# Attention weights turned as pairs of 64 rows, in a two-layer retention and neighbourhood-attention transformer

## The chip, the cores and the metric

The kernel runs on one NeuronCore of a Trainium2 chip. The metric is the device time of one execution in microseconds; a kernel's time is the median of several executions. The core has five engines that work side by side and wait for each other by semaphores: TensorE (PE in the profile; its weight loads are PEld), VectorE (DVE), ScalarE (ACT), GpSimd (POOL) and SyncE (SP, which here only issues loads). TensorE writes to PSUM, which has eight banks of 512 fp32 columns on 128 partitions; VectorE and ScalarE take results out of it.

## What is computed

A transformer of two layers on 256 latent and 256 context tokens of width 1024. Layer 0 mixes by retention, layer 1 by attention: 32 heads of width 32, where each latent token attends to a window of latent tokens with a learned bias and to all context tokens. An MLP of width 4096 follows each mixer, with layer norms and modulation in between. The part that matters here, cut from the reference:

```python
def row_block(args):
    q_r, r = args
    ...
    s_loc = jnp.einsum('bqhd,bikhd->bhqik', q_r, k_band).astype(jnp.float32) + bias
    s_ctx = jnp.einsum('bqhd,blhd->bhql', q_r, k_c).astype(jnp.float32)
    s = jnp.concatenate([s_loc.reshape(b, nh, GRID_W, band), s_ctx], axis=-1)
    prob = jax.nn.softmax(s, axis=-1).astype(v.dtype)
    p_loc = prob[..., :band].reshape(b, nh, GRID_W, kh, GRID_W)
    return (jnp.einsum('bhqik,bikhd->bqhd', p_loc, v_band)
            + jnp.einsum('bhql,blhd->bqhd', prob[..., band:], v_c))
```

## The kernel before

Every matrix product is done to nearly fp32 precision by three TensorE passes (`mm3`): each operand is rounded to fp32r (`hi`, by ScalarE) and the rest is kept (`lo`, by subtraction on VectorE or GpSimd), and hi x hi, hi x lo and lo x hi are summed in PSUM. Weights come as units of 512 KB: `fetch` issues SP's load into one of four `raw` buffers and ScalarE's rounding, `lows` the subtraction. A unit is usable when both are done, and its `raw` buffer is free for another load then.

The attention of layer 1 is cut into 16 tiles, n = 0 to 15: four heads (group n // 2) and half of the queries (128 of 256; n % 2). A tile passes through these stages:

- `scores(n)`: TensorE multiplies queries by keys for four heads side by side, 32 rows of the array each, into four PSUM banks (`pqk`).
- `soften(n)`: for each head VectorE adds the bias to the scores and takes the minimum (scores are negated), and ScalarE takes the exponential and its sum, into `s` in SBUF (128 queries x 416 keys: 160 near, 256 far). Its end issues the bias load of tile n+2 on GpSimd's queue.
- `invert(n)`: VectorE takes the reciprocals of the sums and spreads them (`rr`).
- the turn, `flip_near(n)` and `flip_far(n)`: TensorE transposes the weights (`ppt`), keys to the partitions. The near part is turned in halves of 64 queries: eight transposes of 64 rows, two row halves of the array at a time, into two banks. The far part is eight transposes of 128 rows into two more banks, and `rr` is transposed (one of 128 rows) into the right half of attend's bank. ScalarE copies one near and one far bank to SBUF, VectorE the others. `turned(n)` is ScalarE's copy of the turned reciprocals, at the head of the next step.
- `attend(n)`: TensorE multiplies the turned weights by the values (`pav`, 32 columns of the array for each head), VectorE multiplies by the reciprocals (`rt`), ScalarE rounds the result (`oTh`) and VectorE subtracts (`oTl`).

The loop over `STEPS` (lines 1893 to 1917) runs these as a pipeline: step n does the scores and softening of tile n+2, one block of other TensorE work (`before`: a group of keys `K`, queries `Q`, a quarter of the second half's values `V`, or the first half of an output projection `W`), the turn of tile n+1 and attend of tile n. `before` leaves a function that takes its result out of PSUM (`evac`; for keys two ScalarE roundings and two VectorE subtractions), run between the near and the far part. The step's entry names its weight units: `early` ahead of the scores, `late` behind the softening, `last` at the end. In steps 1 to 8 their subtractions are GpSimd's, later mostly VectorE's.

In this stretch TensorE, VectorE, ScalarE and GpSimd are held to the order in which the program is written (`on`: each instruction is pinned behind the one written before it on its engine); the pinning of ScalarE lasts beyond the loop, to the first blocks of the MLP. A bank or a buffer is taken by the next tile when the last reader of the one before has finished. One bank is attend's throughout, a second from step 13, and the output projections hold one each from their block on.

Of the kernel before, what the change touches and what calls it, by code (L numbers as in the profile page):

```python
# [10 lines left out]
F32 = mybir.dt.float32  # L11
# [6 lines left out]
P = 128  # L18
# [75 lines left out]
def kernel(  # L94
# [23 lines left out]
    pe, act, dve, pool, sp = (  # L118
        InOrder(tc, getattr(nc, e), e in PIN)
        for e in ("tensor", "scalar", "vector", "gpsimd", "sync")  # L120
    )
# [3 lines left out]
    smp = ec(tc.tile_pool(name="smp", bufs=4))  # L125
# [15 lines left out]
    def nm(s):  # L141
        uid[0] += 1
        return f"{s}_{uid[0]}"

    def bank(s="ps"):
        return psp.tile([P, 512], F32, tag="ps", name=nm(s))
# [8 lines left out]
    def tsl(t):  # L155
        return slice(t * P, (t + 1) * P)
# [82 lines left out]
    def fetch(n, home=None):  # L239

        for src, k, ncol in specs[len(units) : len(units) + max(n, 0)]:
            raw = rawp.tile([P, k, ncol], F32, tag="raw", name=nm("raw"))
            sp.dma_start(out=raw[:], in_=src.rearrange("(k p) n -> p k n", p=P))
            if home is None:
                hi = hip.tile([P, k, ncol], F32R, tag="hi", name=nm("hi"))
                lo = lop.tile([P, k, ncol], F32R, tag="lo", name=nm("lo"))
            else:
                both_ = slot(home, [P, 2, k, ncol], F32R, "unit")
                hi, lo = both_[:, 0], both_[:, 1]
            act.copy(out=hi[:], in_=raw[:])  # L250
            pending.append((lo[:], raw[:], hi[:]))
            units.append((hi, lo))
# [23 lines left out]
    def lows(n=100, eng=None):  # L276
        for lo, raw, hi in pending[:n]:
            (eng or dve).tensor_sub(out=lo, in0=raw, in1=hi.bitcast(F32))
        del pending[:n]
# [21 lines left out]
    def cv(name, p0=0, p1=P):  # L301
        o, w = CONST_COLS[name]
        if o < NC0:
            return cst0[p0:p1, o : o + w]
        return cst1[p0:p1, o - NC0 : o - NC0 + w]

    ident = cv("ident")
# [403 lines left out]
    def residual(t, xn, gb, eng=None):  # L711
        if eng:
            eng.tensor_mul(out=R[t], in0=xn, in1=gb[:, 0, :])
            eng.tensor_add(out=R[t], in0=R[t], in1=gb[:, 1, :])
            return
        pool.on = True
        pool.tensor_mul(out=R[t], in0=xn, in1=gb[:, 0, :])
        pool.tensor_add(out=R[t], in0=R[t], in1=gb[:, 1, :])
        pool.on = False
# [218 lines left out]
    for i in range(4):  # L938
        k = 2 * i
# [140 lines left out]
    for h in range(RH):  # L1080
# [11 lines left out]
        else:  # L1092
# [13 lines left out]
            for u in range(4):  # L1106
                ((wh, wl),) = take(1)
                for t in range(4):
                    for kk in range(2):
                        k = 2 * u + kk  # L1110
# [75 lines left out]
        for t in range(4):  # L1186
            po = bank("po")
            scs = list(range(4)) if t < 2 else [2, 3]
            for i, sc in enumerate(scs):
                a, b = S[sc]  # L1190
# [8 lines left out]
                out=on, in0=po[:], scalar1=mv[:, 0:1], scalar2=r[:], op0=ALU.subtract, op1=ALU.mult  # L1199
# [7 lines left out]
        def to_oT(t):  # L1207
            pT = bank("pT")
            for i in range(4):
                pe.transpose(pT[:, tsl(i)], gs[:, t, tsl(i)], ident)  # L1210
            pv_ = pT[:].rearrange("p (k t) -> p k t", k=4)
            act.copy(out=oh[:, :, tsl(t)], in_=pv_)
            dve.tensor_sub(out=ol[:, :, tsl(t)], in0=pv_, in1=oh[:, :, tsl(t)].bitcast(F32))

        between = {4: lambda: to_oT(0), 5: lambda: to_oT(1)}
# [31 lines left out]
        else:  # L1247
# [17 lines left out]
            def turn(t):  # L1265
                return [mod_pt(xns[t], half) for half in range(2)]
# [78 lines left out]
    for hf in range(2):  # L1345
# [60 lines left out]
        for half in range(2):  # L1406
# [68 lines left out]
            p = turn(0)  # L1475
# [9 lines left out]
            p = turn(1)  # L1485
# [13 lines left out]
    NS = 16  # L1499
# [117 lines left out]
    NEARK, FARK = NEAR * ROWS, NLAT  # L1617
# [18 lines left out]
    sums, rrs, Es, pss = {}, {}, {}, {}  # L1636

    def scores(n):

        g, qt = n // 2, n % 2  # L1640
        pss[n] = [bank("pqk") for _ in range(4)]
        q, k = q_of(g), kTs[g // 2][:, g % 2]
        if qt == 0:
            spans = [(0, slice(0, NEARK)), (NEARK, slice(NLAT, NT))]
        else:
            spans = [(0, slice(NLAT - NEARK, NT))]
        for o, keys in spans:
            for i, (a, b) in enumerate(((0, 0), (0, 1), (1, 0))):
                for j in range(4):
                    js = slice(32 * j, 32 * j + 32)  # L1650
                    pe.matmul(
                        pss[n][j][:, o : o + keys.stop - keys.start], lhsT=q[js, a, tsl(qt)], rhs=k[js, b, keys],
                        start=(i == 0), stop=(i == 2), tile_position=(32 * j, 0),
                    )
# [28 lines left out]
    def av_half(n):  # L1683
        return av[n == NS - 2][:, 256 * (n % 2) : 256 * (n % 2) + 256]

    def invert(n):

        rr = rrs[n] = smp.tile([P, 4, HD], F32, tag="rr", name=nm("rr"), bufs=1)
        dve.reciprocal(out=sums[n][:], in_=sums[n][:])
        dve.tensor_copy(out=rr[:], in_=sums[n][:].unsqueeze(2).broadcast_to([P, 4, HD]))  # L1690

    def near_part(n):
        return turnedP[n % 2][:, :512].rearrange("p (a h t) -> p a h t", a=2, h=4)

    def far_part(n):
        return turnedP[n % 2][:, 512:1536].rearrange("p (h k t) -> p h k t", h=4, k=2)

    def flip_near(n):
        pn = [bank("ppt") for _ in range(2)]
        for j in range(4):  # L1700
            for a in range(2):
                qs = slice(64 * a, 64 * a + 64)
                pe.transpose(
                    pn[a][:, 64 * j : 64 * j + 64], Es[n, j][qs, 32 * a : 32 * a + P], ident[qs, qs],
                    tile_position=(64 * a, 0),
                )
        for a in range(2):
            (dve.tensor_copy if a else act.copy)(
                out=near_part(n)[:, a], in_=pn[a][:, :256].rearrange("p (h t) -> p h t", h=4)
            )  # L1710

    def flip_far(n):
        for a in range(2):
            pf = bank("ppt")
            for i in range(4):
                c0 = NEARK + P * (i % 2)
                pe.transpose(pf[:, tsl(i)], Es[n, 2 * a + i // 2][:, c0 : c0 + P], ident)
            (dve.tensor_copy if a else act.copy)(
                out=far_part(n)[:, 2 * a : 2 * a + 2], in_=pf[:].rearrange("p (h k t) -> p h k t", h=2, k=2)
            )  # L1720
        pe.transpose(av_half(n)[:, P:], rrs[n][:].rearrange("p h d -> p (h d)"), ident)

    oTs = [None]
    rts = {}

    def turned(n):

        rts[n] = smp.tile([P, P], F32, tag="rt", name=nm("rt"), bufs=2)
        act.copy(out=rts[n][:], in_=av_half(n)[:, P:])

    def attend(n, between=lambda: None):

# [39 lines left out]
    def wo_add(half, t):  # L1772
        add_to(t, half, gated(wops[half, t], t, half, G1), dve)
# [65 lines left out]
    soften(1)  # L1839
    v_part(0, 1)  # L1840
    invert(0)
    flip_near(0)
    flip_far(0)
    residual(1, xns[1], gb, dve)
    regrid()
    v_part(0, 2)
# [10 lines left out]
    def Q(p):  # L1857
        def f():
            for u in range(2):
                q_mm(p, u)  # L1860
            return lambda: q_evac(p)

        return f
# [18 lines left out]
        ((), (), W01, (None,)),  # L1882
        ((), (), W10, ()),
    ]
    pool.on = True

    def weights(homes, eng=None):
        for home in homes:
            fetch(1, home)
            if eng:  # L1890
                lows(1, eng)

    for n, (early, late, before, last) in enumerate(STEPS):
        turned(n)
        weights(early, pool if n else None)
        scores(n + 2)
        soften(n + 2, lambda: lows(0 if n else 1))
        if n > 9:
            lows(1)
        weights(late, pool if n < 9 else dve if n == 9 else None)  # L1900
        if n == 9:
            Q(3)()()
            weights((None,), dve)
        evac = before()
        flip_near(n + 1)
        if evac:
            evac()
        if n == NS - 3:
            av[1] = bank("pav")
        flip_far(n + 1)  # L1910
        if n == NS - 3:
            turned(n + 1)
        attend(n)
        invert(n + 2)
        if n == 10:
            wo_add(0, 0)
        weights(last, pool if n < 9 else None)


    n = NS - 1  # L1920
    st1 = small(smp, 24, "st1", name="st1", bufs=1).rearrange("p (q s) -> p q s", q=4)
    weights((N_Q, N_B))
    attend(n - 1, lambda: lows(1))
    flip_near(n)
    flip_far(n)
    turned(n)
    lows(2)
    us = take(4, 0)
    gb = slot(N_K1, [P, 2, D], F32, "gb")
# [302 lines left out]
```

## Time and profile before

| what | us |
|---|---|
| median of 3 runs | 1175.21 (1174.76 to 1175.26) |
| the profiled execution, device time | 1176.4 |
| its span, first to last instruction | 1174.6 |
| TensorE busy | 1162.7 |
| VectorE busy | 812.9 |
| ScalarE busy | 480.3 |
| GpSimd busy | 145.3 |

The attention loop runs from 842.96 us (scores of tile 2) to about 964.8 us of the span, the turn of the first tile stands ahead of it at 830.54 us, that of the last behind it at 965.69 us. A row of the timeline reads: start, length, engine, line, operation, what is written from what, partitions and elements, count; in brackets the time that the engine stood idle before it and what ended that. Consecutive instructions of one kind are merged in one row, so a row's length is from the first one's start to the last one's end; matmuls overlap, and the distance between starts is their pace. All lines are L84, the helper that pins instructions, so groups are told apart by their tiles.

### The profile page before, as it was taken

Reading aid. Unit: us, or ns where it says so; the run is one execution under the profiler, and the core shown is the slowest. Engines: PE = TensorE matmul, PEld = TensorE weight load, DVE = VectorE, ACT = ScalarE, POOL = GpSimd, SP = SyncE. Lnnn points to the kernel's source line nnn. Section 1 sums busy time; section 2 is a strip of 40 time slices with the busy share of each in tenths; the row PEclk is TensorE's granted clock in tenths of the full one; section 3 lists DMA queues with packets and bytes.
Section 4 is the critical chain, followed back from the end, with each engine's and each line's share of the span. In section 5 each row is a group of like instructions: output and inputs, shape, how many; then the busy total and the mean of one; then the engine's idle time right before and its main releaser. Section 6 shows DMA issues by size and latency. Waiting matters only on the chain.

```text
span 1174.6 us, 17876 instructions
## 1 busy us (share of the span) xinstructions
PE 1162.7 (99%) x7042; PEld 982.2 (84%) x7042; DVE 812.9 (69%) x1286; ACT 480.3 (41%) x816; POOL 145.3 (12%) x168
## 2 busy tenths in 40 slices
PE   9999999999999999999999999999999999999997
PEld 6788888888888889888788878889778879999886
DVE  3575896689697376468888665578465588877555
ACT  3643442143323245232222433237466675655450
POOL 0102002100200240000202000140245300000000
PEclk9999999999999999999999999999999999999999
DMA  9742552857255214347675655646634543676861
GB/s 322 233 135 79 162 177 77 288 154 220 85 158 189 76 57 133 79 119 226 233 228 180 199 192 183 197 143 197 200 110 150 168 132 120 202 242 220 289 218 37
DMA packets 134468, 199.99 MB, mean 170 GB/s; under 512 B 16192, under 2 KB 76384, under 8 KB 134384
## 3 DMA queue, kind: packets, MB, share of 16 engines
q1 hardware_dynamic: 129696, 185.64, 49.9%
q0 software_dynamic: 3296, 10.55, 2.9%
q10 hardware_dynamic: 1392, 2.67, 0.6%
q8 instruction: 55, 0.90, 0.3%
q14 instruction: 29, 0.24, 0.1%
HBM read 190.31 MB, written 10.61 MB: 171 GB/s over the span
## 4 chain that ended last, share of the span: by engine, by line
PE 92%; DVE 4%; DMA 2%; ACT 1%; issue 1%; DVEq 0%; ACTq 0%; SPq 0%
PE p L84 39%; PE pw L84 7%; PE pv L84 7%; PE pq L84 7%; PE pg L84 7%; PE pn L84 6%; PE pnv L84 4%; PE po L84 3%; PE pnw L84 2%; PE ppt L84 2%; PE pS L84 1%; DVE acc L84 1%; PE pav L84 1%; PE pqk L84 1%; PE pt L84 1%; DMA rawa<-in_ada_w_dram 1%
## 5 line engine op out<-in xcount | busy, mean ns | idle before, releaser
L84 ACT CAST hi<-raw 128x1024 fp32r<-128x1024 f32 (+1 forms) x222 | 220.7, 1011 | 287.1 <-DMA raw<-in_mlp_w_dram 118.2
L84 DVE TENSOR_TENSOR lo<-raw,hi 128x1024 fp32r<-128x1024 f32 (+1 forms) x211 | 247.0, 1184 | 86.9 <-ACT hi L84 85.2
L84 PE MATMUL p<-hi,hid 128*128 128x512 f32 (+1 forms) x792 | 230.9, 373 | 0.0
L84 PE MATMUL p<-hTh,hi 128*128 128x256 f32 (+1 forms) x512 | 168.6, 330 | 0.0
L84 PE MATMUL p<-hTh,lo 128*128 128x256 f32 (+1 forms) x512 | 168.1, 330 | 0.4 <-DVE lo L84 0.4
L84 PEld LDWEIGHTS p<-hi,hid 128*128 128x128 f32 x792 | 144.9, 188 | 26.2
L84 PE MATMUL p<-hTl,hi 128*128 128x256 f32 (+1 forms) x512 | 166.2, 329 | 0.0
L84 PE MATMUL p<-lo,hid 128*128 128x512 f32 (+1 forms) x396 | 147.4, 372 | 0.0
L84 DVE SCALAR_TENSOR_TENSOR acc<-rawa,scol,acc 128x1024 f32<-128x1024 f32 x63 | 83.4, 1344 | 44.7 <-DMA rawa<-in_ada_w_dram 44.6
L84 PEld LDWEIGHTS p<-hTh,lo 128*128 128x128 f32 x512 | 97.3, 190 | 9.6 <-DVE lo L84 0.9
L84 PEld LDWEIGHTS p<-hTh,hi 128*128 128x128 f32 x512 | 97.3, 190 | 8.7
L84 PEld LDWEIGHTS p<-hTl,hi 128*128 128x128 f32 x512 | 96.3, 190 | 8.7
L84 PEld LDWEIGHTS p<-lo,hid 128*128 128x128 f32 x396 | 74.6, 188 | 12.9
L84 ACT CAST hid<-r 128x512 fp32r<-128x512 f32 (+1 forms) x60 | 31.2, 520 | 108.2 <-DVE r L84 108.1
L84 DVE SCALAR_TENSOR_TENSOR strips<-rawa,scol,strips 128x512 f32<-128x512 f32 x84 | 57.5, 744 | 0.0
L84 DVE TENSOR_TENSOR hid<-r,hid 128x512 fp32r<-128x512 f32 (+1 forms) x60 | 33.8, 563 | 25.5 <-ACT hid L84 25.5
L84 PE MATMUL pw<-hi,oh 128*128 128x512 f32 x128 | 50.9, 398 | 0.0
L84 PE MATMUL pg<-hi,hTh 128*128 128x512 f32 x128 | 50.7, 396 | 0.0
L84 PE MATMUL pv<-hi,hTh 128*128 128x512 f32 x128 | 50.4, 394 | 0.0
L84 PE MATMUL pw<-hi,ol 128*128 128x512 f32 x128 | 49.9, 390 | 0.0
L84 PE MATMUL pg<-hi,hTl 128*128 128x512 f32 x128 | 49.9, 390 | 0.0
L84 PE MATMUL pv<-hi,hTl 128*128 128x512 f32 x128 | 49.9, 390 | 0.0
(234 smaller groups left out, 2200.3 us busy)
## 6 DMA issues: line engine op xcount, KB each, us to landing
raw<-in_mlp_w_dram SPq DMA_DIRECT2D x128, 512.0 KB
rawa<-in_ada_w_dram SPq DMA_DIRECT2D x80, 512.0 KB
raw<-in_ret_w_in_dram SPq DMA_DIRECT2D x46, 512.0 KB
raw<-in_nat_w_in_dram SPq DMA_DIRECT2D x24, 512.0 KB
rawq<-in_ada_w_dram SPq DMA_DIRECT2D x16, 512.0 KB
raw<-in_ret_w_o_dram SPq DMA_DIRECT2D x16, 512.0 KB
rpb_near<-far SPq DMA_DIRECT2D x20, 256.0 KB
bias<-rpb_near POOLq DMA_DIRECT2D x16, 320.0 KB, 3.6
```

The costliest lines, as they stand in the source:

```text
L84: r = f(*args, **kwargs)
```

## The change

- `flip_near`, `flip_far` and `turned` become one function `flip`. The far part is turned in halves of 64 rows too, sixteen transposes instead of eight, each row half into a bank of its own; all four banks are taken at the head. The reciprocals are turned as two halves of 64 rows into the near banks, columns 256 to 320, between the near and the far part, and copied at once, one half by ScalarE and one by VectorE. With `late` (first and last tile) their transposes and copies come behind the far copies.
- `evac` runs between the near and the far copies (`between`), in steps 9 and 11 ahead of all copies of the turn.
- Of `late` only the first unit (in step 9 both) is rounded ahead of `before`; the second behind the turn. Steps 1, 2 and 4 have such a second unit.
- From step 10 on, the VectorE subtraction that followed the softening stands behind the turn's copies.
- Attend's second bank is taken behind the turn of step 13 instead of within it.
- ScalarE is no longer pinned from the end of the loop on.

```diff
--- before.py
+++ after.py
@@ -1695,38 +1695,49 @@
     def far_part(n):
         return turnedP[n % 2][:, 512:1536].rearrange("p (h k t) -> p h k t", h=4, k=2)
 
-    def flip_near(n):
+    HALVES = [slice(64 * a, 64 * a + 64) for a in range(2)]
+    rts = {}
+
+    def flip(n, between=lambda: None, late=False):
+
         pn = [bank("ppt") for _ in range(2)]
+        pf = [bank("ppt") for _ in range(2)]
+        rr = rrs[n][:].rearrange("p h d -> p (h d)")
+        rts[n] = smp.tile([P, P], F32, tag="rt", name=nm("rt"), bufs=2)
+        copies = act.copy, dve.tensor_copy
+
+        def turn_half(o, src, a):
+            pe.transpose(o, src, ident[HALVES[a], HALVES[a]], tile_position=(64 * a, 0))
+
+        def reciprocals():
+            for a in range(2):
+                turn_half(pn[a][:, 256:320], rr[HALVES[a], :], a)
+
+        def copy_reciprocals():
+            for a in range(2):
+                copies[a](out=rts[n][:, HALVES[a]], in_=pn[a][:, 256:320])
+
         for j in range(4):
             for a in range(2):
-                qs = slice(64 * a, 64 * a + 64)
-                pe.transpose(
-                    pn[a][:, 64 * j : 64 * j + 64], Es[n, j][qs, 32 * a : 32 * a + P], ident[qs, qs],
-                    tile_position=(64 * a, 0),
-                )
+                turn_half(pn[a][:, 64 * j : 64 * j + 64], Es[n, j][HALVES[a], 32 * a : 32 * a + P], a)
+        if not late:
+            reciprocals()
         for a in range(2):
-            (dve.tensor_copy if a else act.copy)(
-                out=near_part(n)[:, a], in_=pn[a][:, :256].rearrange("p (h t) -> p h t", h=4)
-            )
-
-    def flip_far(n):
+            copies[a](out=near_part(n)[:, a], in_=pn[a][:, :256].rearrange("p (h t) -> p h t", h=4))
+        if not late:
+            copy_reciprocals()
+        for i in range(8):
+            c0 = NEARK + P * (i % 2)
+            for a in range(2):
+                turn_half(pf[a][:, 64 * i : 64 * i + 64], Es[n, i // 2][HALVES[a], c0 : c0 + P], a)
+        between()
         for a in range(2):
-            pf = bank("ppt")
-            for i in range(4):
-                c0 = NEARK + P * (i % 2)
-                pe.transpose(pf[:, tsl(i)], Es[n, 2 * a + i // 2][:, c0 : c0 + P], ident)
-            (dve.tensor_copy if a else act.copy)(
-                out=far_part(n)[:, 2 * a : 2 * a + 2], in_=pf[:].rearrange("p (h k t) -> p h k t", h=2, k=2)
-            )
-        pe.transpose(av_half(n)[:, P:], rrs[n][:].rearrange("p h d -> p (h d)"), ident)
+            copies[a](out=far_part(n)[:, :, :, HALVES[a]], in_=pf[a][:].rearrange("p (h k t) -> p h k t", h=4, k=2))
+        if late:
+            reciprocals()
+            copy_reciprocals()
 
     oTs = [None]
-    rts = {}
-
-    def turned(n):
-
-        rts[n] = smp.tile([P, P], F32, tag="rt", name=nm("rt"), bufs=2)
-        act.copy(out=rts[n][:], in_=av_half(n)[:, P:])
 
     def attend(n, between=lambda: None):
 
@@ -1839,8 +1850,7 @@
     soften(1)
     v_part(0, 1)
     invert(0)
-    flip_near(0)
-    flip_far(0)
+    flip(0, late=True)
     residual(1, xns[1], gb, dve)
     regrid()
     v_part(0, 2)
@@ -1882,7 +1892,7 @@
         ((), (), W01, (None,)),
         ((), (), W10, ()),
     ]
-    pool.on = True
+    pool.on = act.on = True
 
     def weights(homes, eng=None):
         for home in homes:
@@ -1891,39 +1901,37 @@
                 lows(1, eng)
 
     for n, (early, late, before, last) in enumerate(STEPS):
-        turned(n)
         weights(early, pool if n else None)
         scores(n + 2)
         soften(n + 2, lambda: lows(0 if n else 1))
-        if n > 9:
-            lows(1)
-        weights(late, pool if n < 9 else dve if n == 9 else None)
+        spread = 1 if n < 9 else 2
+        weights(late[:spread], pool if n < 9 else dve if n == 9 else None)
         if n == 9:
             Q(3)()()
             weights((None,), dve)
         evac = before()
-        flip_near(n + 1)
-        if evac:
+        if evac and n in (9, 11):
             evac()
+            evac = None
+        flip(n + 1, evac or (lambda: None))
+        if n > 9:
+            lows(1)
+        weights(late[spread:], pool)
         if n == NS - 3:
             av[1] = bank("pav")
-        flip_far(n + 1)
-        if n == NS - 3:
-            turned(n + 1)
         attend(n)
         invert(n + 2)
         if n == 10:
             wo_add(0, 0)
         weights(last, pool if n < 9 else None)
+    act.on = False
 
 
     n = NS - 1
     st1 = small(smp, 24, "st1", name="st1", bufs=1).rearrange("p (q s) -> p q s", q=4)
     weights((N_Q, N_B))
     attend(n - 1, lambda: lows(1))
-    flip_near(n)
-    flip_far(n)
-    turned(n)
+    flip(n, late=True)
     lows(2)
     us = take(4, 0)
     gb = slot(N_K1, [P, 2, D], F32, "gb")
```

## The prediction

> **What bounds the kernel now.** I read the head of the page and its chain that ended last first, then the timeline of one middle attention step on every engine.
>
> ```profile
> span 1174.6 us, 17876 instructions
> PE 1162.7 (99%) x7042; PEld 982.2 (84%) x7042; DVE 812.9 (69%) x1286; ACT 480.3 (41%) x816; POOL 145.3 (12%) x168
> PE 92%; DVE 4%; DMA 2%; ACT 1%; issue 1%; DVEq 0%; ACTq 0%; SPq 0%
> ```
>
> TensorE holds 92% of the chain and is busy 99% of the span: a microsecond taken off its stream is a microsecond won, as long as VectorE (DVE) and ScalarE (ACT) still deliver. The change touches the 14 steps of the attention loop and the two turns outside it. Step n=1 turns its weights at 858.30; I count t from there.
>
> ```profile
> 858.30 0.34 PE L84 MATMUL ppt<-cst,s 64*128 64x64 f32 x4
> 858.30 0.46 PE L84 MATMUL ppt<-cst,s 64*128 64x64 f32 x8
> 858.69 1.09 PE L84 MATMUL ppt<-cst,s 128*128 128x128 f32 x8
> 859.62 0.27 PE L84 MATMUL pav<-cst,rr 128*128 128x128 f32 x1
> 859.83 0.43 PE L84 MATMUL pav<-pt,natv 128*32 128x128 f32 x8
> 860.62 0.96 PE L84 MATMUL pqk<-kT,qT 32*128 32x160 f32 x24
> 861.51 0.50 PE L84 MATMUL pn<-hTh,hi 128*128 128x512 f32 x1
> ```
>
> The first two rows are the near part, cut after two pairs and after four. Two more pairs cost 0.46 - 0.34 = 0.12, so 0.06 a pair. The far part (eight 128-row transposes) and the reciprocals (one) run from 858.69 to 859.62, about 0.11 each. From the first transpose to attend's first matmul is 1.53. No matmul here waits: the blocks follow each other. What runs beside them:
>
> ```profile
> 857.04 1.98 ACT L84 CAST hi<-raw 128x1024 fp32r<-128x1024 f32 x2
> 858.92 0.36 ACT L84 COPY pt<-ppt 128x256 f32<-128x256 f32 x1
> 859.19 0.84 ACT L84 CAST kT<-pn 128x256 fp32r<-128x256 f32 x2
> 859.93 0.57 ACT L84 COPY pt<-ppt 128x512 f32<-128x512 f32 x1
> 861.86 0.30 ACT L84 CAST oTh<-rt 128x128 fp32r<-128x128 f32 x1 [1.36 <-DVE rt L84]
> 862.07 0.26 ACT L84 COPY rt<-pav 128x128 f32<-128x128 f32 x1
> 863.94 0.65 ACT L84 ACTIVATE s<-s,mn 128x416 f32<-128x416 f32 x1 [1.61 <-DVE mn L84]
> 858.16 4.73 POOL L84 TENSOR_TENSOR lo<-raw,hi 128x1024 fp32r<-128x1024 f32 x2 [1.08 <-ACT hi L84]
> 858.83 0.43 DVE L84 COPY pt<-ppt 128x256 f32<-128x256 f32 x1 [2.81 <-PE ppt L84]
> 862.19 0.85 DVE L84 TENSOR_TENSOR oTl<-rt,oTh 128x128 fp32r<-128x128 f32 x1 [0.37 <-ACT oTh L84]
> 863.31 0.58 DVE L84 CUSTOM_DVE_ANT_1 s<-pqk,bias 128x416 f32<-128x416 f32 x1
> 863.82 0.58 DVE L84 CUSTOM_DVE_ANT_1 s<-pqk,bias 128x416 f32<-128x416 f32 x1
> ```
>
> VectorE has slack in such a step (2.81 idle before its near copy), ScalarE little: its near copy starts right behind the two casts.
>
> **The shorter turn.** After the change a turn is thirteen pairs in one form: four near, one of reciprocals, eight far. The fourth pair starts at t = 0.46 - 0.22 (one transpose's tail) = 0.24, the thirteenth at 0.24 + 9 x 0.0625 = 0.80. The next form starts 0.15 behind the last pair, as the far part does now (0.39 - 0.24), so attend begins at t = 0.96 instead of 1.53: **0.57 a turn**. If the switch to attend's form costs the 0.21 that it takes now (859.62 to 859.83) it is 0.52. Fourteen turns of the loop: -8.0 (-7.3 at least).
>
> **The copies.** ACT's copy of the reciprocals (0.26 for 128x128) goes; ACT and DVE each get a 128x64 one. No row shows that form: it costs more than nothing and less than the 0.26; from the near copy's spacing (0.27 for 256 columns, 858.92 to 859.19) I take 0.17 on ACT and 0.13 on DVE. Alone this is hidden, but it lies between the near copy and the release of the near banks.
>
> **The moved unit** (steps 1, 2 and 4, the ones with two late units before step 9). ACT in step 1 becomes: near copy at t = 0.57, half copy, two key casts (0.74), far copy (0.5), then the second cast at t = 2.3, then oTh. The trace shows what POOL's subtraction does to oTl meanwhile: the row above took 0.85 while `lo` ran (858.16 to 862.89) and ended 0.15 behind it; the same operation with POOL idle:
>
> ```profile
> 853.33 0.29 DVE L84 TENSOR_TENSOR oTl<-rt,oTh 128x128 fp32r<-128x128 f32 x1 [0.36 <-ACT oTh L84]
> ```
>
> So oTl stands still until POOL's subtraction ends. The Trainium skill, page "SBUF — State Buffer", section "Who interferes with whom", says the same of a VectorE instruction with two SBUF inputs against a GpSimd instruction that reads SBUF: the later one blocks fully; the trace agrees (0.85 against 0.29). Now POOL ends at t = 4.6. With the cast moved, POOL's second subtraction starts 1.12 behind the cast's start (as 858.16 stands to 857.04), at t = 3.4, and takes 2.38; oTh comes out of ACT 1.24 behind the cast's start, so oTl always finds POOL at work, and ends at t = 5.9 instead of 4.74. Behind oTl on DVE are the reciprocals and the next scores' bias and minimum; ACT's exponentials wait for those. They began at t = 5.64; they will begin at 6.8, with the next turn at 8.3 instead of 8.8. Four at 0.63 end 1.0 behind the next turn's start. One cast (0.94) precedes the near copy, which then starts at 2.0, and its half copy ends at 2.45. The scores want four PSUM banks at 0.96 + 0.80 = 1.75: eight banks, less attend's, less the key result's, less four of the turn, leaves two; DVE's near bank is the third, ACT's the fourth. **Wait 0.7** in step 3, then 0.5 more for the K matmuls' bank (ACT's far copy ends at 3.75; they want it at 3.2). Step 2's moved unit does it again with the lateness carried over: 1.0 + 0.7 in step 4. In step 5 the fourth bank is a query result's, evacuated by DVE behind ACT at t = 2.3: 0.6. And step 5's values need the late unit and its successor:
>
> ```profile
> 884.90 4.75 POOL L84 TENSOR_TENSOR lo<-raw,hi 128x1024 fp32r<-128x1024 f32 x2 [1.08 <-ACT hi L84]
> 890.11 2.41 POOL L84 TENSOR_TENSOR lo<-raw,hi 128x1024 fp32r<-128x1024 f32 x1 [0.46 <-ACT hi L84]
> 888.18 0.50 PE L84 MATMUL pnv<-hi,hTh 128*128 128x512 f32 x1
> 892.62 0.44 PE L84 MATMUL pnv<-lo,hTh 128*128 128x512 f32 x1
> ```
>
> The subtraction of 890.11 ends at 892.52, and PE uses its result at 892.62 (0.05 late, a row of 0.44 instead of 0.39): no slack. With its predecessor at t = 3.5 to 5.9 it runs 5.9 to 8.3. PE starts the values at 0.96 + 0.80 + 0.77 (scores) + 0.6 = 3.1 and uses it 4.4 later (892.62 - 888.18), at 7.5: 0.75. Together **+4.25**.
>
> **The short steps** (10, 12, 13; 11 takes their lateness over).
>
> ```profile
> 953.51 0.51 PE L84 MATMUL pnw<-hi,oTh 128*128 128x512 f32 x1
> 956.43 0.34 PE L84 MATMUL ppt<-cst,s 64*128 64x64 f32 x4
> 962.63 0.28 PE L84 MATMUL ppt<-cst,s 64*128 64x64 f32 x2
> 962.70 0.63 ACT L84 ACTIVATE s<-s,mn 128x416 f32<-128x416 f32 x1
> 963.32 0.35 ACT L84 COPY pt<-ppt 128x256 f32<-128x256 f32 x1
> ```
>
> DVE per step, from one start to the next: four softenings (0.51 each, 863.31 to 863.82), near, half and far copies (0.34, 0.13, 0.6), one `lo` (1.2), multiplication, oTl, reciprocals (0.8), 0.4 waiting for oTh: 5.5. PE: 2.92 of matmuls (953.51 to 956.43) + 0.96 + 0.80 + 0.8 = 5.5. They draw level, and `lo` now lies behind the far copy, ahead of attend's multiplication, which pushes the softening 0.3 to 1.2 later. Once the softening is that late the near copies release their banks late too: waits of 0.2 to 0.6 at four places in steps 11 to 13, **+1.3**, an estimate. Keys first (steps 9, 11) is what keeps this small: behind the copies as now, 0.9 more. Elsewhere it moves nothing.
>
> **The two ends.** In step 13 the exponentials end 0.69 behind the turn's start (963.32 - 962.63); 0.8 later, ACT's copies for attend(14) (0.27 + 0.17 + 0.6) end at 2.6, PE wants them at 1.75: **+0.8**. The last turn has its reciprocals behind the copies, in the near banks, so PE waits for both near copies:
>
> ```profile
> 965.69 1.49 PE L84 MATMUL ppt<-cst,s 64*128 64x64 f32 x16
> 967.04 0.48 PE L84 MATMUL pnw<-unit,oTh 128*128 128x512 f32 x1
> 966.58 1.22 DVE L84 TENSOR_TENSOR lo<-raw,hi 128x1024 fp32r<-128x1024 f32 x1
> 968.13 1.01 DVE L84 COPY pt<-ppt 128x256 f32<-128x256 f32 x2
> 830.54 1.49 PE L84 MATMUL ppt<-cst,s 64*128 64x64 f32 x16
> 831.41 0.59 ACT L84 COPY flat<-pnv 128x512 f32<-128x512 f32 x1 [0.57 <-PE ppt L84]
> 831.89 0.87 ACT L84 COPY pt<-ppt 128x256 f32<-128x256 f32 x2
> 831.89 0.48 PE L84 MATMUL pnv<-hi,hTh 128*128 128x512 f32 x1
> ```
>
> DVE's near copy starts 2.44 behind this turn (968.13 - 965.69), held by `lo` and oTl; say 2.2 to 2.6 + 0.2 for pair and switch afterwards: PE goes on 2.8 behind the turn's start instead of 1.35: **+1.45**. In the first turn ACT's near copy stands behind `flat`, which waits for the far transposes; it ends at about 832.02, so PE goes on at 832.24 instead of 831.89: **+0.35**. ScalarE is no longer held to program order behind the loop; that can cost or save up to one cast (0.94), taken as 0.
>
> **Sum.** -8.0 + 4.25 + 1.3 + 0.8 + 1.45 + 0.35 = +0.15. It is made on the profiled execution, 1176.4 long with a span of 1174.6; the median of the runs is 1175.21, 1.2 less, and the difference carries over: **1175.4**.
>
> **Rivals.** *The lock does not reach PE* (faster): softening late, yet the banks come free in time; then 1.2 + 1.7 + 0.6 of the waits go, and the time is 1171.9. For it: DVE's slack of 2.81, and none of these waits stands in the trace now. Against: ACT's near copy already starts with no idle time before it. *The fourth bank is a far copy's* (slower): all four banks of a turn are now taken at its head, and if the next scores get ACT's far bank instead of a near one, they wait until t = 2.35 against 1.75 in the undisturbed steps too, and longer in the late ones: 0.6 in steps 0 to 2 and 6, some 0.5 more in 3 to 5, 3.9 in all: 1179.3. It decides from the point where the far copy ends behind 1.75; now it ends at 860.50, 0.12 ahead of the scores, so the trace allows either bank. Against: the near banks are free first. *Weight loads set the pace* (the change does not do what it says): at 0.11 a transpose, as the 128-row ones have now, 26 of them take 2.9 instead of 1.5, 1.4 a turn more, some 1195 in all. The x8 row of 0.46 speaks against it. The Trainium skill, page "TensorE: Matmul & The Clock Gate", section "LDWEIGHTS (loading the stationary operand)", gives a load as its columns by 1.2, 107 ns here whatever the rows, which would be this case; the trace has eight loads and transposes of 128 columns in 0.46, so loads of the two row halves overlap.
>
> **How the numbers follow.** Forecast 0.46 (1173.4 to 1177.5), lock hidden 0.33, far bank 0.19, loads 0.02. About 0.2%, 2.35 us, can be told from no change: faster is below 1172.86, slower above 1177.56. Faster 0.33, same 0.46, slower 0.21. The range takes in the faster rival, the dearer switch (+0.7), a ScalarE cast either way and part of the slower rival: 1171.7 to 1178.3.
>
> **What would show it.** One form of transpose, 26 a turn, attend 0.95 behind the first: right about the saving. oTl of steps 1, 2 and 4 over 2 us long, and PE waiting before the scores of steps 3 to 5: right about the lock. PE waiting 1.5 or more between the last turn's far pairs and its reciprocals: right about the end. Scores in step 1 already waiting for ACT's far copy: the second rival. The forecast is wrong if oTl is late and PE is not, or if the turn takes over 1.1.

## The result, and the profile after

| | median, us | runs, us | ratio to the kernel before |
|---|---|---|---|
| before | 1175.21 | 1174.76 to 1176.14 | |
| changed | 1181.38 | 1179.74 to 1183.16 | 1.0054 [1.0043, 1.0065] |

The brackets give the 95% interval of the ratio. The change costs 6.2 us, half a per cent (5.1 to 7.6 by the interval); it was forecast at +0.2 with 1178.3 as the upper end. The head of the changed kernel's page and its chain:

```profile
span 1178.0 us, 18186 instructions
PE 1158.4 (98%) x7186; PEld 977.5 (83%) x7186; DVE 822.7 (70%) x1302; ACT 478.5 (41%) x816; POOL 146.1 (12%) x168
PE 91%; DVE 4%; ACT 3%; DMA 1%; issue 1%; POOL 0%; DVEq 0%; ACTq 0%; SPq 0%
```

TensorE is busy 4.3 us less than before (1162.7), in a span 3.4 longer: the turns became cheaper, and 7.7 us of waiting came in. ScalarE's share of the chain rose from 1% to 3%. The turn itself, from TensorE's timeline in step 1 (start, length, what):

```profile
856.39 0.46 PE L84 MATMUL ppt<-cst,s 64*128 64x64 f32 x8
856.69 0.23 PE L84 MATMUL ppt<-cst,rr 64*128 64x64 f32 x2
856.75 0.67 PE L84 MATMUL ppt<-cst,s 64*128 64x64 f32 x16
857.35 0.43 PE L84 MATMUL pav<-pt,natv 128*32 128x128 f32 x8
```

Attend begins 857.35 - 856.39 = 0.96 behind the first transpose, as forecast; before it was 1.53, so a turn saves 0.57. The waits, from the same timeline, the brackets giving the idle time and its releaser:

```profile
867.13 0.90 PE L84 MATMUL pqk<-kT,qT 32*128 32x416 f32 x10 [0.19 <-ACT rt L84]
...
876.72 1.02 PE L84 MATMUL pqk<-kT,qT 32*128 32x160 f32 x22 [0.62 <-ACT rt L84]
...
892.25 0.51 PE L84 MATMUL pnv<-lo,hTh 128*128 128x512 f32 x1 [0.66 <-POOL lo L84]
...
896.91 0.95 PE L84 MATMUL pqk<-kT,qT 32*128 32x160 f32 x21 [1.20 <-ACT flat L84]
...
959.38 0.90 PE L84 MATMUL pqk<-kT,qT 32*128 32x416 f32 x10 [1.18 <-ACT rt L84]
...
966.27 0.54 PE L84 MATMUL pav<-pt,R 128*32 128x128 f32 x16 [1.28 <-ACT pt L84]
...
969.22 0.27 PE L84 MATMUL ppt<-cst,rr 64*128 64x64 f32 x1 [0.95 <-DVE pt L84]
...
981.03 1.09 PE L84 MATMUL pt<-cst,xn 128*128 128x128 f32 x8 [0.65 <-ACT xn L84]
```

Scores wait for the near banks (`ACT rt` is ScalarE's copy of the reciprocals out of one), the values of step 5 for POOL's subtraction, attend(14) for a far copy. Set block by block against the profile of before (the distance between the starts of the same blocks in the two profiles, and how it changes), the change comes to:

| place | forecast | in the profile |
|---|---|---|
| fourteen turns of the loop | -8.0 | -8.0 |
| first turn | +0.35 | +0.4 |
| steps 3 to 5 | +4.25 | +3.8 |
| scores of steps 6 and 7 | 0 | +1.8 |
| attend in step 8 | 0 | +0.5 |
| steps 10 to 13 | +1.3 | +3.1 |
| attend(14) | +0.8 | +1.4 |
| last turn | +1.45 | +1.0 |
| behind it (the first layer norm), and small differences elsewhere | 0 | +1.1 |
| sum | +0.15 | +5.1 |

The span shows only 3.4 of the 5.1 because the profiled execution of before had lost 0.9 at 559 us and 0.7 at 684 us, long ahead of the change; no later profile has both. And this profiled execution is the shortest run of the changed kernel: the others take up to 3.4 us more. Part of that is a second loss, told below.

### The profile page after: what moved, and what is told of

Its sections match the earlier page's. It is cut to its first block, busy times and chain, and to the rows that moved or that the text cites. A ratio compares the mean times of both kernels' runs of the same rounds, so it can differ in the third digit from the quotient of the medians.

```text
span 1178.0 us, 18186 instructions
## 1 busy us (share of the span) xinstructions
PE 1158.4 (98%) x7186; PEld 977.5 (83%) x7186; DVE 822.7 (70%) x1302; ACT 478.5 (41%) x816; POOL 146.1 (12%) x168
## 4 chain that ended last, share of the span: by engine, by line
PE 91%; DVE 4%; ACT 3%; DMA 1%; issue 1%; POOL 0%; DVEq 0%; ACTq 0%; SPq 0%
PE p L84 44%; PE pw L84 7%; PE pv L84 7%; PE pq L84 7%; PE pg L84 7%; PE pn L84 5%; PE pnv L84 3%; PE po L84 3%; PE pS L84 1%; ACT s L84 1%; PE pt L84 1%; PE pnw L84 1%; PE p1t L84 1%; PE pada L84 1%; PE pqk L84 1%; ACT hi L84 1%
## 5 line engine op out<-in xcount | busy, mean ns | idle before, releaser
L84 ACT ACTIVATE s<-s,mn 128x416 f32<-128x416 f32 x64 | 40.4, 633 | 32.1 <-DVE mn L84 32.1
```

Of the source, the lines that this page charges most:

```text
L84: r = f(*args, **kwargs)
```

## The experiments

Every kernel was timed against the kernel before on the same chip (1175.1 to 1175.4 there). A ratio is known to about 0.1%, 1.1 us, to either side. So the waits are also compared block by block in the profiles, as in the table above; there a difference of 0.1 can be seen.

| run | what it is | median | ratio |
|---|---|---|---|
| e1 | changed, ScalarE pinned as before | 1182.01 | 1.0052 [1.0038, 1.0066] |
| e2 | changed, unit not moved | 1179.39 | 1.0033 [1.0021, 1.0046] |
| e3 | changed, moved unit's subtraction on VectorE | 1179.56 | 1.0038 [1.0025, 1.0051] |
| e4 | before, far part in halves of 64 only | 1173.11 | 0.9984 [0.9975, 0.9993] |
| e5 | changed, subtractions of steps 10 to 13 early | 1183.58 | 1.0064 [1.0052, 1.0077] |
| e6 | e1, last reciprocals as before | 1179.23 | 1.0033 [1.0021, 1.0046] |
| e7 | new turn and keys first alone | 1173.16 | 0.9982 [0.9973, 0.9991] |
| e8 | e7 without keys first | 1173.60 | 0.9990 [0.9981, 0.9998] |
| e9 | e7 and the moved unit | 1177.25 | 1.0015 [1.0006, 1.0024] |
| e10 | e7, first reciprocals as before too | 1172.13 | 0.9973 [0.9963, 0.9983] |
| e11 | e10, step 1's unit moved, subtracted by VectorE | 1172.62 | 0.9976 [0.9966, 0.9985] |
| e12 | e7, last reciprocals late | 1175.41 | 1.0003 [0.9994, 1.0012] |
| e13 | e5, ScalarE pinned | 1179.30 | 1.0040 [1.0028, 1.0051] |
| e14 | e9, moved unit's subtraction on VectorE | 1174.72 | 0.9999 [0.9990, 1.0008] |

### e1: ScalarE pinned

```diff
         weights(last, pool if n < 9 else None)
-    act.on = False
```

> The changed kernel with ScalarE held to program order behind the loop too, as before the change. Theory A (the freed ScalarE is a cost that was put at nothing: in the changed kernel one weight cast of 0.95 us stands ahead of step 13's exponentials, one of 0.95 between the last two copies that attend(14) waits for, and a cast that waits for a load stands ahead of oTh of tile 15): PE's wait of 1.28 in attend(14) falls below 0.3, the wait of 0.65 before the first transposes of the layer norm behind the loop goes, the span falls by 2 to 3 us, and the runs lie within 1.5 us of each other instead of 3.4: 1178 to 1179 us. Theory B (the end is late because the short steps are late, whatever ScalarE's order): under 0.7 us less, 1180.7 to 1181.4.

Theory A fell as far as the time goes: 1182.0, which is above theory B's range too. The waits in attend(14) and ahead of the layer norm do go, but most of that time comes back in the last turn (2.17 us idle there instead of 0.95), whose reciprocals wait for the near copies (e6 tries that). What the profile showed instead was the granted clock. Two windows of it, 3.41 us each, from the view by windows (busy time of PE, PEld, DVE, ACT, POOL, then the granted clock, DMA share, GB/s):

```profile
895.83:899.24 3.41, 2.21 (x43) 1.62 (x32) 1.14 (x3) 2.78 (x8) 2.33 (x2) 1.00 0.38 102
899.24:902.65 3.41, 3.41 (x9) 2.69 (x9) 2.30 (x9) 1.99 (x6) 0.83 (x2) 0.50 0.49 142
```

In the first, TensorE is busy 2.21 of 3.41: step 6's wait of 1.20. In the next the clock is at half for the whole window, a dip, and 3.41 us of matmuls do the work of 1.7. Another such window lies at 970.92, behind the last turn's wait. In this kernel's five runs the mean clock tells them apart: 1179.5 and 1180.0 at 0.998, 1182.0, 1182.4 and 1183.7 at 0.994 to 0.995.

### e2: the unit not moved

```diff
-        spread = 1 if n < 9 else 2
+        spread = 2
```

> The changed kernel with both late units of steps 1, 2 and 4 rounded and subtracted ahead of the turn again, all else as changed. Theory A (the moved unit, by POOL's subtraction standing over oTl and the reciprocals, makes the waits of 0.7 to 1.5 us in steps 3 to 6): oTl is at most 0.9 us long, those waits go, and 4.5 to 5.5 us with them: 1176 to 1177. Theory B (the steps are too short for VectorE and ScalarE once each has lost 0.57 us, wherever the unit stands): the waits come back in other places, 1 to 2 us less: 1179.4 to 1180.4.

At the edge of theory B by the median, 2.0 under the changed kernel. Its profiled execution has two dips of the clock in it and took 1180.65:

```profile
956.04:959.45 3.41, 2.23 (x20) 1.54 (x17) 3.00 (x10) 3.41 (x10) 0.00 (x0) 1.00 0.14 26
959.45:962.86 3.41, 3.41 (x10) 2.40 (x8) 1.58 (x8) 3.28 (x9) 0.00 (x0) 0.50 1.01 360
...
966.28:969.69 3.41, 1.89 (x36) 1.44 (x29) 3.12 (x9) 1.50 (x5) 0.00 (x0) 1.00 0.54 157
969.69:973.10 3.41, 3.41 (x10) 2.67 (x9) 2.35 (x3) 1.05 (x1) 0.00 (x0) 0.50 0.73 217
```

Step 6's wait is gone, but steps 2, 3 and 5 still lose 0.5, 1.2 and 1.2, 3.1 with step 4: those waits belong to the shorter turn, not to the move. Steps 2 to 7 lose 5.7 in the changed kernel, so 2.6 is what the move itself adds there. The waits of the shorter turn are seen best in e7, below.

### e3: the moved unit's subtraction on VectorE

```diff
-        weights(late[spread:], pool)
+        weights(late[spread:])
         ...
         attend(n)
+        if late[spread:]:
+            lows(1)
         invert(n + 2)
```

> The changed kernel with the unit still moved, but its subtraction done by VectorE behind oTl instead of by GpSimd beside it. Theory A (the lock between POOL's subtraction and VectorE's oTl and rr is what delays the softening): oTl back to 0.3 us, VectorE late by one subtraction of 1.2 at most, waits of steps 3 to 6 fall to a third: 1177 to 1178. Theory B (ScalarE's order is what delays it: the near copy behind a cast, oTh behind another): the waits stay, within 1 us of the changed kernel: 1180.4 to 1182.4.

1179.56 lies between the two ranges. The waits of steps 3 to 5 did shrink (1.1 to 0.65, 1.3 to 0.8, and 0.9 to 0.25 in step 5's values), so the lock is part of the cost; step 6's 1.2 stayed. e14 repeats it where nothing else is in the way.

### e4: halves of 64 rows in the far part, nothing else

```diff
-            pe.transpose(pf[:, tsl(i)], Es[n, 2 * a + i // 2][:, c0 : c0 + P], ident)
+                pe.transpose(pf[a][:, 64 * i : 64 * i + 64], Es[n, i // 2][qs, c0 : c0 + P], ident[qs, qs],
+                    tile_position=(64 * a, 0))
```

> The kernel before with one edit: the far part is turned in halves of 64 rows, each into a bank of its own; the reciprocals, the moved unit, the orders of VectorE and ScalarE stay as before. The far part's eight transposes of 0.11 become eight pairs of 0.0625, 0.4 us less a turn, but the switch of form now stands ahead of the reciprocals instead of ahead of the far part. Theory A (what was lost is the rest of the change): 16 turns by 0.3 to 0.4, 5 to 6 us less than before: 1169 to 1171. Theory B (any shorter turn meets waits for the banks and the copies): half or less is kept, 1172.5 to 1175.

Theory B: 2 us less, no window dips. Each turn of the loop gives 0.37 in its profile, the two outside it 0.3 to 0.4, 5.9 in all; 3.2 of that is spent in waits of 0.3 to 1.0 in steps 3, 5, 10, 11, 12 and 13.

### e5 and e13: the subtractions of steps 10 to 13 early, ScalarE free and pinned

```diff
+        if n > 9:
+            lows(1)
         spread = 1 if n < 9 else 2
         ...
         flip(n + 1, evac or (lambda: None))
-        if n > 9:
-            lows(1)
```

> The changed kernel with VectorE's subtraction of steps 10 to 13 back ahead of the turn's copies. Theory A (behind the far copy it holds attend's multiplication and with it ScalarE's two casts and the next exponentials by 1.2 us, which makes step 13's wait of 1.18 us): that wait falls to 0.1 to 0.4, and those behind it, in attend(14) and the last turn, by about 1 together: 2 us less, and one dip of the clock fewer: 1178 to 1179.5. Theory B (the near copies are late in any order): the wait stays over 0.9, 1180.5 to 1182.

The mechanism was right: step 13's wait fell from 1.18 to 0.30. The time was not: 1183.6 is outside both ranges, and e5 is the slowest kernel of all. ScalarE's timeline in e5, at the last turn:

```profile
965.43 0.32 ACT L84 CAST oTh<-rt 128x128 fp32r<-128x128 f32 x1
969.62 1.04 ACT L84 CAST unit<-raw 128x1024 fp32r<-128x1024 f32 x1 [3.87 <-DMA raw<-in_mlp_w_dram]
970.57 0.29 ACT L84 CAST oTh<-rt 128x128 fp32r<-128x128 f32 x1
970.77 0.85 ACT L84 COPY pt<-ppt 128x256 f32<-128x256 f32 x2
```

and TensorE's:

```profile
971.19 0.76 PE L84 MATMUL ppt<-cst,rr 64*128 64x64 f32 x2 [3.82 <-ACT pt L84]
...
974.60 0.63 PE L84 MATMUL pnw<-hi,oTh 128*128 128x512 f32 x1
975.02 0.63 PE L84 MATMUL pnw<-lo,oTh 128*128 128x512 f32 x1
...
976.46 0.40 PE L84 MATMUL pnw<-hi,oTl 128*128 128x512 f32 x1
976.69 0.40 PE L84 MATMUL pnw<-hi,oTh 128*128 128x512 f32 x1
```

A weight cast that waits 3.87 us for its load stands ahead of the last turn's copies, so TensorE stands still for 3.82; two windows at half clock (969.28 to 976.10) follow, the first of them beginning within this wait. In them a matmul takes 0.42 (974.60 to 975.02) instead of 0.23 (976.46 to 976.69). Whether the freed ScalarE was the loss was tried by pinning it again:

> The changed kernel with VectorE's subtractions of steps 10 to 13 early and ScalarE pinned behind the loop. Theory A (the parts add up, and the freed ScalarE was the loss of the run with early subtractions alone): 1173.2 + 4.1 + 2.25 = 1179.5, within 1 us, and PE's wait in the last turn falls from 3.8 to 1.2 to 1.6. Theory B (early subtractions themselves make the end late when the reciprocals stand behind the copies): the wait stays over 2.5, 1182 to 1184.

It was: 1179.3, and a wait of 1.24 in the last turn. So the freed ScalarE costs nothing that can be told where other things are late (e1 against the changed kernel), and 4.3 us by the medians where its list happens to put a waiting cast first. One of e5's five runs, at 1179.7, does not have the loss.

### e6 and e12: the last tile's reciprocals

```diff
+        if late is None:
+            pe.transpose(av_half(n)[:, P:], rr, ident)
         ...
+        if late is None:
+            act.copy(out=rts[n][:], in_=av_half(n)[:, P:])
         ...
-    flip(n, late=True)
+    flip(n, late=None)
```

> The changed kernel with ScalarE pinned behind the loop and the last tile's reciprocals turned as one transpose of 128 rows into attend's bank, as before. Theory A (the last turn's wait of 2.17 in the pinned kernel is the near banks', held by the copies that stand behind the subtraction and oTl): that wait goes, 1.5 to 2.5 us, and with it the dip at 970: 1178 to 1179.5. Theory B (PE waits there for something else that is late, the softening): it shows up as a wait ahead of the projections, under 0.7 less: above 1180.5.

1179.23, 2.8 less than e1: theory A. The same part alone, on e7:

> The new turn with keys first, and the last tile's reciprocals in the near banks behind the copies, as in the change; all else in order. Theory A (the near copies of the last turn stand behind a subtraction and oTl on VectorE, whatever the steps before): PE waits 1.2 to 2.2 us there, 1174.5 to 1175.5, and in runs where the wait falls into one clock window, 1.7 more. Theory B (the wait comes from the lateness of steps 10 to 13, which is not here): under 0.5, 1173 to 1173.7.

Theory A again, 2.25 more than e7. TensorE's timeline of e12 at the last turn, and the windows behind it:

```profile
962.96 0.96 PE L84 MATMUL ppt<-cst,s 64*128 64x64 f32 x24
965.16 0.67 PE L84 MATMUL ppt<-cst,rr 64*128 64x64 f32 x2 [1.24 <-ACT pt L84]
965.75 0.73 PE L84 MATMUL pnw<-unit,oTh 128*128 128x512 f32 x2
```

```profile
963.18:966.59 3.41, 2.05 (x30) 1.57 (x27) 3.27 (x8) 2.53 (x6) 0.00 (x0) 1.00 0.41 123
966.59:970.00 3.41, 3.41 (x10) 2.63 (x9) 1.91 (x2) 0.00 (x0) 0.00 (x0) 0.50 0.73 236
```

From the first transpose to the projection is 965.75 - 962.96 = 2.79; the prediction had 2.8. In the changed kernel itself it is 969.42 - 967.07 = 2.35, behind the wait in attend(14). The near copies are late as forecast, VectorE's behind `lo` and oTl; ScalarE's, which ends the wait of 1.24, stands behind two weight casts and the oTh that oTl waits for:

```profile
962.65 1.99 ACT L84 CAST unit<-raw 128x1024 fp32r<-128x1024 f32 x2
964.55 0.29 ACT L84 CAST oTh<-rt 128x128 fp32r<-128x128 f32 x1
964.75 0.85 ACT L84 COPY pt<-ppt 128x256 f32<-128x256 f32 x2
```

The dip behind the wait is what the prediction did not have.

### e7 and e8: the new turn alone, keys first or not

```diff
-        spread = 1 if n < 9 else 2
+        if n > 9:
+            lows(1)
+        spread = 2
         ...
-    act.on = False
-    flip(n, late=True)
+    flip(n, late=None)
```

The diff is against the changed kernel, with `late=None` as in e6; e8 also leaves out the call of `evac` ahead of the turn in steps 9 and 11.

> Of the change only the new turn (thirteen pairs, reciprocals in the near banks, four banks at once) and the keys first in steps 9 and 11; the moved unit, VectorE's order of steps 10 to 13, the last turn's reciprocals and ScalarE's pinning as before the change. If the three undone parts are what cost, 14 turns by 0.57 less the waits of steps 2 to 5 (3.1 in the run without the moved unit): 1171 to 1173. If the near banks' longer hold by the reciprocals is a cost of its own: slower than the kernel with far halves only, 1173.5 to 1176.

> The same with the keys between the near and the far copies in steps 9 and 11 too. If keys first saves what the forecast says (0.9 us), it is 0.5 to 1.2 slower than the kernel beside it; if keys first only holds up the near copies, the waits of steps 10 and 12 fall and it is 0.3 to 0.8 faster.

1173.16 and 1173.60, each just outside the first range given for it. Against the kernel before 2 us are won. Keys first is worth 0.4 by the medians, which these intervals can't tell from nothing; in the profiles the scores of steps 10 and 12 wait 0.7 longer without it. The turn of e7 is 0.2 shorter than that of e4, 2.8 over the loop, and yet the two kernels take the same time (1173.16 and 1173.11). Of the 2.8, 1.1 is lost in the first turn, whose reciprocals come late in e7 alone, and the rest in longer waits. Of the 8.0 saved in the loop, 3.0 are spent in steps 2 to 5, 0.4 in step 8 and 2.0 in steps 10 to 13, with none of the other parts of the change there. TensorE's timeline of e7 shows where in steps 3 and 5, ScalarE's in step 4 why:

```profile
868.22 0.91 PE L84 MATMUL pqk<-kT,qT 32*128 32x416 f32 x10 [0.33 <-ACT rt L84]
869.43 0.50 PE L84 MATMUL pn<-hTh,hi 128*128 128x512 f32 x1 [0.30 <-ACT pt L84]
...
886.80 0.84 PE L84 MATMUL pqk<-kT,qT 32*128 32x416 f32 x9 [0.66 <-DVE qT L84]
```

```profile
883.21 1.98 ACT L84 CAST hi<-raw 128x1024 fp32r<-128x1024 f32 x2
885.09 0.36 ACT L84 COPY pt<-ppt 128x256 f32<-128x256 f32 x1
885.36 0.20 ACT L84 COPY rt<-ppt 128x64 f32<-128x64 f32 x1
885.46 1.09 ACT L84 ACTIVATE qT<-pn 128x256 fp32r<-128x256 f32 x2
```

ScalarE has two casts (1.98) between the exponentials and its near copy. TensorE now arrives 0.57 earlier and waits for whatever comes behind them: a near bank in step 3, the query result's in step 5. For step 2 a run supports it: in e11, where one cast of step 1 is moved away, its wait of 0.5 goes. For the others, steps 10 to 13 among them, the cause is read from the timelines alone.

### e9 and e14: the moved unit on the clean base

e9 is e7 with `spread = 1 if n < 9 else 2` again, e14 is e9 with the edit of e3.

> The new turn with keys first (the kernel of 1173.16 us), and the moved unit put back, subtracted by GpSimd as in the change. Theory A (oTl and rr stand still behind POOL's subtraction; the softening is late; steps 3 to 7 wait 2.9 us more than without the move, as in the two profiles without and with it): 1175.5 to 1176.5 where no clock window dips, with a wait of 1.2 ahead of step 6's scores that drops the clock to half for 3.4 us in some runs, 1.7 us each. Theory B (the move costs only because the later steps are late too): under 1 us more, 1173 to 1174.2.

> The new turn with keys first and the moved units, their subtraction by VectorE behind oTl. Theory A (the lock is most of the move's 4.1): 1173.8 to 1174.8. Theory B (ScalarE's order is most of it: the moved cast pushes the next steps' casts and with them the subtraction of step 5, which then meets rr; the lock over oTl is a third to a half): 1175 to 1176.2.

By the medians the move costs 4.1 us; theory A in both, though e9 came out above its range. The profiles, neither of which has a dip, give less: against e7 steps 3 to 7 of e9 wait 3.0 longer, as theory A has it, and step 2 waits 0.5 less, so the move's own is 2.5. In e9's profile the first turn, ahead of the move, also waits 0.7 longer, and four of its eleven runs have a mean clock of 0.996 or less, against 0.999 in the profiled one. So the rest of the 4.1 is not shown to be the move's waits.

VectorE's timeline of e7 (unit not moved), of e9 and of e14, each in step 4, and at the end GpSimd's of e14:

```profile
889.34 0.23 DVE L84 COPY rr<-sums 128x128 f32<-128x128 f32 x1
```

```profile
889.83 2.12 DVE L84 TENSOR_TENSOR oTl<-rt,oTh 128x128 fp32r<-128x128 f32 x1 [0.37 <-ACT oTh L84]
...
892.07 2.20 DVE L84 COPY rr<-sums 128x128 f32<-128x128 f32 x1
```

```profile
887.19 0.29 DVE L84 TENSOR_TENSOR oTl<-rt,oTh 128x128 fp32r<-128x128 f32 x1 [0.37 <-ACT oTh L84]
...
888.74 2.21 DVE L84 COPY rr<-sums 128x128 f32<-128x128 f32 x1
```

```profile
888.19 2.68 POOL L84 TENSOR_TENSOR lo<-raw,hi 128x1024 fp32r<-128x1024 f32 x1 [2.08 <-ACT hi L84]
```

With the subtraction on VectorE oTl is back at 0.29, and 2.5 of the 4.1 us are back by the medians (1.4 of the 2.5 in the profiles). What is left is the second row: `rr`, a copy of 0.23 in e7 and the last thing of step 4, stands 2.2 us beside POOL's subtraction of the next unit, makes step 5's softening late, and with it `flat` and the scores of step 6 (1.20). The Trainium skill, page "SBUF — State Buffer", section "Who interferes with whom", says that a copy between SBUF tiles can take the port pair shared with GpSimd as well; 2.2 against 0.23 agrees.

### e10 and e11: towards a better kernel

e10 turns the first tile's reciprocals too into attend's bank (`flip(0, late=None)`); e11 adds the moved unit in step 1 alone, with its subtraction on VectorE.

> The new turn with keys first, and the first tile's reciprocals too turned as one transpose of 128 rows into attend's bank. Theory A (the wait of 0.89 in the first turn is the near bank's, held by ScalarE's copy behind flat): it goes, 0.7 to 1.1 us less: 1172.0 to 1172.5. Theory B (PE waits there for something that is late anyway): within 0.3 of 1173.16.

> The same, and the second late unit of step 1 alone moved behind the turn, its subtraction by VectorE behind oTl. Theory A (with the lock out of the way the move does what it is for: ScalarE's near copy comes one cast of 0.95 earlier in step 1, and the waits of 0.5 in step 2 and 1.2 in step 3 shrink by 0.5 to 1 together): 1171.2 to 1172. Theory B (the cast only comes to stand in another's way): no gain, 1172 to 1173.5.

e10 is the fastest kernel of the study: 3 us under the kernel before, 9 under the changed one. The 1.0 against e7 is more than the first turn's forecast of 0.35, but e10's first turn is also 0.37 shorter than that of the kernel before. In nine of the twelve profiles with the late reciprocals the first turn costs 0.4 against before, in e6, e7 and e9 0.75, 0.7 and 1.4. In e9 the exponential ahead of ScalarE's copies came late, because VectorE had waited 4.21 us for a transfer (`lat_v`); in the changed kernel that wait is 2.68. e11 gains nothing: the wait of step 2 goes, that of step 3 grows.

## Why the prediction was wrong

The saving came as forecast, and what it cost the other engines did not. The parts, each by the difference of two medians, and by what the two profiles lose where the part acts (in the loop and the last turn; in steps 2 to 7; from step 12 on; in the last turn), dips of the clock left out:

| part | runs | medians | profiles |
|---|---|---|---|
| new turn with keys first | e7 against before | -2.0 | -2.5 |
| moved unit | e9 against e7 | +4.1 | +2.5 |
| late subtractions in steps 10 to 13 | e6 against e9 | +2.0 | +2.0 |
| last tile's late reciprocals | e12 against e7 | +2.25 | +1.8 |

By the medians they add to 1175.2 - 2.0 + 4.1 + 2.0 + 2.25 = 1181.5; the changed kernel takes 1181.4. That they meet within 0.1 is partly luck: each difference is uncertain by more than 1 us, and the first three add to e6's median whatever they are. What the sum tests is that the last part adds to the others; e13, which lacks the late subtractions, tests it again (1179.3 against 1179.5).

- **The shorter turn** was right in mechanism and size: 0.96 long, 0.57 a turn.
- **What is late once the turn is short** is the step that failed first. The working put steps 0 to 9 at no wait but those of the move. With no unit moved (e7) steps 2 to 5 lose 3.0 us and step 8 another 0.4. In steps 3 and 5 that stands behind ScalarE's two casts; the quoted row of 857.04 with its 1.98 showed them, with the near copy starting right behind.
- **The moved unit** was put at 4.25 in steps 3 to 5, and the changed kernel loses 3.8 there. The agreement is in part luck. The lock over oTl was right, and so were the waits of step 4 and of step 5's values, 1.1 and 1.0 more in e9 than in e7. But the waits of step 3 and of step 5's scores come without the move too, and are shorter with it. The move's other cost, the lock over `rr` at the end of step 4, which makes the scores of step 6 lose 1.5, was not in the working: the price given for a late softening stopped at oTl.
- **Short steps and late subtractions**: +1.3 forecast, +3.1 in the profile. 2.0 of it comes with the subtractions early too (e7), where the working put all of it down to their being late. The late subtraction adds 1.1 in steps 12 and 13 and 0.9 at and behind the last turn: behind the far copy it holds attend's multiplication, oTh behind it, ScalarE's two casts behind that and so the next exponentials. Keys first was put at 0.9 and measures 0.4 by the medians, 0.7 in the profiles.
- **The ends**: the last turn costs 1.45 in e12 and e13, the very figure of the forecast, for the reason given; in the changed kernel it costs 1.0. The first turn's 0.35 is right in most profiles.
- **ScalarE free behind the loop** was put at nothing, either way by one cast. As a sum that holds in e1, but in e5 it cost 4.3, so the bound was not one: a cast can bring its load's wait with it.
- **The clock** was not in the working at all. The granted clock was 1.00 all through the loop in the profile of before, so a microsecond of waiting was priced at one; a wait of 1.2 or more can cost 1.7 on top. Two of the changed kernel's five runs (1182.5 and 1183.2) have a mean clock of 0.996 where the profiled one has 0.998. Two more lie 1.6 us above the profiled one at the same 0.998. They have no profile; between the profiles there are, the first 100 us, where the code is the same in all, differ by up to 3.1 us, so these two need have nothing to do with the change.

Of the rivals, the lock did reach TensorE (against the first), the scores of step 1 do not wait (against the far bank), and the transposes keep 0.0625 a pair (against the weight loads). As this is less than the 0.11 of one 128-row transpose, two loads side by side do not explain the pace by themselves; what sets it was not tried. The slower side was given 0.21, by the wrong mechanism.

## What to carry to other kernels

Shortening the bound engine moves every other engine's deadline at once: before counting the saving, look at each step for the engine that already works without a gap in front of a copy, here ScalarE behind two casts. A saving can be used up that way: e7 saved 0.2 a turn more than e4 and was no faster. Try the parts of a change one at a time: here one part was worth 2 to 3 us, and three others took 6 to 8 back. And a wait of 1.2 us on a TensorE that otherwise never waits can be dearer than it looks.

## What was not expected of the hardware

The granted clock goes to 0.50 for one window of 3.41 us (two in e5), and the windows of one run lie on a fixed grid of 3.41. In the loop and behind it this was seen nine times in seven profiles, each time behind a window in which TensorE was idle for about 1.2 us or more (the least: 2.23 busy of 3.41 in e2 and e13). It is not certain behind such a window: eight others with as much idle time have no dip behind them. The changed kernel's own profile has one:

```profile
894.16:897.57 3.41, 2.21 (x71) 1.79 (x68) 1.53 (x6) 3.41 (x10) 1.87 (x2) 1.00 0.64 207
897.57:900.98 3.41, 3.41 (x23) 2.72 (x16) 2.89 (x9) 1.44 (x5) 1.79 (x2) 1.00 0.24 40
```

What else decides is left open. Seven of those eight windows hold all 32 matmuls of an attend, and seven of the nine with a dip hold 18 or fewer; whether that matters was not tried. The kernels whose waits are all under 0.9 us (before, e4, e7, e8, e10, e11) show no dip. The Trainium skill, page "TensorE: Matmul & The Clock Gate", section "Part 1: The HAM clock gate (the "warmup" mystery)", has the free-running window of about 3.4 us and the half clock, as here; but its table has the clock fall after at least one idle window, and here windows that were up to two thirds busy were enough.
